# One last block moved ahead in GpSimd's queue, one output pair sent last, one input block evacuated in one go

## The chip, the cores and the metric

The kernel runs on 1 core of one Trainium2 chip. The metric is the time of one execution in microseconds of the device. Times quoted from the profile are from one profiled execution; all others are medians over runs.

The engines are named as in the profile: PE (TensorE, the matrix products), DVE (VectorE), ACT (ScalarE), POOL (GpSimd) and SP (the queue from which all large transfers of this kernel are issued). Each engine takes its instructions strictly in its own order.

## What is computed

A trunk of two layers over 1024 frames of 1024 features, in float32. Layer 0 runs a state-space branch with a gated linear unit and a retention branch side by side and maps both back; layer 1 is a convolution module. A normalization stands ahead of each layer and behind the last.

```python
def rmsnorm(x, g):
    y = x * rsqrt(mean(x * x, axis=-1) + EPS) * g

def mixer_conv(h, ...):                      # layer 1
    a, b, g = split(h @ w_in, 3)
    u = causal_depthwise_conv31(a * sigmoid(b)) + conv_b
    u = (u - mean(u)) * rsqrt(var(u) + EPS) * ln_g + ln_b
    return (silu(u) * silu(g)) @ w_out       # x = x + this; then the final rmsnorm
```

## The kernel before

Features lie on the 128 partitions, so a 1024x1024 matrix is eight feature blocks (`nb` or `kb`, 0 to 7); frames lie along the free axis, in two halves (`h`, 0 and 1) of 512. A float32 product is made of three faster ones: every operand is split into a high part (`zh`, `wh`, rounded) and a low part (`zl`, `wl`, what the rounding left), and `mm3` adds high by high (L181), low by high (L182) and high by low (L183). One output block of one half is thus 24 matmuls in one of three PSUM banks.

Instructions are put in order by a scheduler that works with priorities (`self.at(number)`) and with orders written by hand: under `issue_after(x)` an instruction comes behind `x` in the order. Such a line adds no wait on the chip by itself between instructions of one engine; it only fixes the queue.

Three places matter here.

- **Front.** `u_block(nb)` (L351) takes the first projection out of PSUM: `evac` (L354) multiplies a half of 512 frames by the normalization factor `R` and writes it into the tile `ut`, once for each half, on DVE. The finished `ut` (two buffers) is sent to DRAM as `u_d[nb]` by L364. The PSUM bank is free when `evac` is done, and the buffer of `ut` is free again when its transfer has landed; block 2 uses the buffer of block 0. The products of blocks 0, 1 and 2 are already made when `R` is ready, so their evacuations come together.
- **Last normalization of layer 1.** For each feature block of half 1, `conv_scale` (L1612) does: scale by the normalization factor (L1626), subtract the scaled mean (L1631), SiLU on ACT (L1632), multiply by the gate `gl` (L1641), high part on ACT (L1235), low part (L1237). Blocks 3, 5 and 7 are done by POOL on the tiles `co`, the others by DVE on tiles `zz` in PSUM. The last product (`w_out_c`, tiles `mm_oc`) of half 1 needs all eight blocks. The same function adds, for half 0, the squares of its finished blocks on POOL (L1678, tile `s2q`); their sum goes through PE (L487, `rf_R`) into the final normalization of half 0. In the order by hand, the additions for blocks 5, 6 and 7 of half 0 come behind the low part of block 3 (`third_low`), and the scaling of block 7 comes behind the low part of block 5.
- **End.** `final_norm` (L1684) multiplies the last 256 frames by their factor and sends them in pairs of feature blocks (L1712), in the order 4-5, 0-1, 2-3, 6-7 of the loop; 4-5 is done by POOL, the other three pairs by DVE.

Of the kernel before, what the change touches and what calls it, by code (L numbers as in the profile page):

```python
# [15 lines left out]
ALU = mybir.AluOpType  # L16
# [3 lines left out]
P = 128  # L20
# [32 lines left out]
class Trunk:  # L53
# [190 lines left out]
    def layer0_front(self, st):  # L244
        tc, nc, A = self.tc, self.nc, self.A
# [36 lines left out]
        for kb in range(KB):  # L282
            t = xt[kb] = ev.tile([P, T], F32, name=f"x_{kb}", tag="xin", bufs=8)
# [67 lines left out]
        def u_block(nb):  # L351
            ut = uv.tile([P, 8, P], F32, name=f"ut_{nb}", tag="ut", bufs=2)

            def evac(h, ps):  # L354
                r = self.R[:, h * HALF:(h + 1) * HALF]
                self.u_evac[nb] = nc.vector.tensor_tensor(
                    ut[:, ::-1, h * 64:(h + 1) * 64], ps[:].rearrange("p (m j) -> p j m", j=8),
                    r.rearrange("p (m j) -> p j m", j=8), op=ALU.mult)
# [5 lines left out]
            nc.sync.dma_start(self.u_d[nb].rearrange("j h g m -> (h g) j m"), ut[:])  # L364
# [874 lines left out]
    def layer0_back_and_layer1(self, st):  # L1239
        nc, A = self.nc, self.A  # L1240
# [101 lines left out]
        for i, x in ((6, t2), (7, t3), (4, t4)):  # L1342
            for m in range(2):
# [268 lines left out]
        def conv_scale(h, Rp, dl):  # L1612
            R, steps = None, {}

            def behind(nb, step, of):

                ins = steps.get((nb - 2, of)) if h and nb in (5, 7) else None
                return self.tc.issue_after(ins.ins) if ins else nullcontext()

            for nb in range(8):  # L1620
                c = cv[h][nb]

                e1, e = (v, gp) if h == 0 else (gp, gp) if nb in (3, 5, 7) else (v, v)
                z = ps_cv.tile([P, HALF], F32, name=f"zz{nb}_{h}", tag="cv") if e is v else c
                with behind(nb, "scale", "sub" if nb == 5 else "low"):
                    e1.tensor_tensor(z[:], c[:], (R if e1 is gp else Rp)[:], op=ALU.mult)  # L1626
                if h and nb == 0:
                    R = lp.tile([P, HALF], F32, name=f"RL_{h}", tag="cq", bufs=1)
                    nc.scalar.copy(R[:], Rp[:])
                with behind(nb, "sub", "gate"):  # L1630
                    steps[nb, "sub"] = e.tensor_tensor(z[:], z[:], dl[:], op=ALU.subtract)  # L1631
                silu = nc.scalar.activation(z[:], z[:], AF.Silu, scale=self.vec(V_LNG, nb), bias=self.vec(V_LNB, nb))  # L1632
                if nb == 0:
                    self.first_silu = silu
                tag, bufs = ("ld", 2) if h == 0 else ("tp", 3) if nb < 3 else ("u", 5)
                g = lp.tile([P, HALF], F32, name=f"gl{nb}_{h}", tag=tag, bufs=bufs)

                with self.tc.issue_after(self.low_load["ca1"].ins) if h == 0 and nb < 2 else nullcontext():
                    nc.sync.dma_start(g[:], self.gs_d[rows(nb), hs(h)])
                with behind(nb, "gate", "low" if nb == 7 else "gate"):  # L1640
                    steps[nb, "gate"] = e.tensor_tensor(z[:], g[:], z[:], op=ALU.mult)  # L1641
# [10 lines left out]
        def w_out_c(h, nb, cols, hold=None):  # L1652

            w = self.wnext(f"woc{nb}_{h}")
            tag, bufs = ("tp", 3) if h and nb > 4 else ("ld", 2)
            xt = lp.tile([P, HALF], F32, name=f"x1l{nb}_{h}", tag=tag, bufs=bufs)
            with self.tc.issue_after(self.early_low.ins) if h and nb > 4 else nullcontext():
                nc.sync.dma_start(xt[:], self.x1_d[rows(nb), hs(h)])
            t = self.opA.tile([P, HALF], F32, name=f"x2_{nb}_{h}", tag=f"A{h}")
            sq = lp.tile([P, HALF], F32, name=f"s2q{nb}_{h}", tag="sacc" if nb == 0 else "ev",  # L1660
                         bufs=1 if nb == 0 else 3)
            final[h].append((t, sq))

            def part(c):
                ps = self.bank(f"mm_oc{nb}_{h}_{c.start}", aux=False)
                n = c.stop - c.start
                self.gemm(ps[:, :n], w, [(a[:, c], b[:, c]) for a, b in zs[h]], hold)
                behind = self.behind.pop(nb, None)
                with self.tc.issue_after(behind.ins) if behind else nullcontext():
                    self.last_add = v.tensor_tensor(t[:, c], ps[:, :n], xt[:, c], op=ALU.add)  # L1670

                with self.tc.issue_after(self.halved.ins) if h == 0 and nb >= N0 else nullcontext():
                    self.squared = nc.scalar.activation(sq[:, c], t[:, c], AF.Square)

                if 0 < nb < KB - (h == 1 and c.start > 0):
                    a = final[h][0][1]
                    with self.tc.issue_after(self.third_low.ins) if h == 0 and nb > 4 else nullcontext():
                        gp.tensor_tensor(a[:, c], a[:, c], sq[:, c], op=ALU.add)  # L1678
                with self.tc.issue_after(self.squared.ins):
                    nc.scalar.mul(t[:, c], t[:, c], self.vec(V_FG, nb))  # L1680
            for c in cols:
                yield part(c)

        def final_norm(h, c):  # L1684
            n = c.stop - c.start
            end = h and c.stop == HALF
# [8 lines left out]
            R = lp.tile([P, HALF], F32, name=f"RF_{h}_{c.start}", tag="dg", bufs=1)  # L1695
            for nb in (4, 5, 0, 1, 2, 3, 6, 7) if end else range(8):
                if nb == 4:
                    yield
# [2 lines left out]
                t = final[h][nb][0]  # L1701
                e = gp if (nb // 2 == 2 if end else nb % 3 == 2) else v
                c0 = h * HALF + c.start
# [5 lines left out]
                    o = lp.tile([P, 2, n], F32, name=f"fo{nb}_{c0}", tag="u", bufs=5)  # L1709
                e.tensor_tensor(o[:, nb % 2, :], t[:, c], (R if e is gp else rp)[:, :n], op=ALU.mult)  # L1710
                if nb % 2:
                    nc.sync.dma_start(self.out[(nb - 1) * P:(nb + 1) * P, c0:c0 + n]  # L1712
                                      .rearrange("(b p) t -> p b t", b=2), o[:])

        with self.at(100000):
            w_out(0, range(8))
# [176 lines left out]
```

## Time and profile before

| | |
|---|---|
| median of 3 runs | 1181.32 us (1181.07 to 1181.44) |
| the profiled execution, its own time | 1181.03 us |
| its span, first to last instruction | 1179.2 us |
| PE busy | 1168.7 us, 99% of the span |
| DVE, POOL, ACT busy | 850.8, 654.2, 489.0 us |
| mean granted TensorE clock | 0.998 |

How to read the views: a row of the timeline has its start and its length in us from the start of the span, then engine, line of the code, operation, tile written `<-` tiles read, shape and count; in brackets how long the engine had been idle before, and what ended that. A row with x2 or more merges neighbours. Matmuls overlap: each is shown for 0.39 us or so, but the next starts about 0.23 us after it. DVEq, SPq and the like are an engine's sequencer.

### The profile page before, as it was taken

To read this page: it belongs to the slowest core of one execution; us is meant where nothing else is said; L and a number is where in the kernel's file an instruction comes from. 1 tells how busy PE (TensorE), PEld (TensorE's weight loads), DVE (VectorE), ACT (ScalarE), POOL (GpSimd) and SP (SyncE) were. 2 spreads that over 40 slices of the span, in tenths; PEclk is the share of its full clock that TensorE was granted. 3 is DMA by queue.
4 is the path that set the end of the run, shared out by engine and by line. 5 is a ranking of instruction groups with operands and counts; after the bars stand their busy time and mean duration, and the time that the engine had idled before them with its cause. 6 is when DMAs were issued, how large, how long until landed. Compare 5 with 4: busy or idle time off the path is not lost.

```text
span 1179.2 us, 17214 instructions
## 1 busy us (share of the span) xinstructions
PE 1168.7 (99%) x6286; PEld 978.4 (83%) x6286; DVE 850.8 (72%) x1464; ACT 489.0 (41%) x719; POOL 654.2 (55%) x448
## 2 busy tenths in 40 slices
PE   9999999999999999999999999999999999999997
PEld 7888888888888888999888888888888888888776
DVE  7975698777417359586679333599999899899834
ACT  6322232322223231333456324455536675444763
POOL 2059999888145344232673111588534567677653
PEclk9999999999999999999999999999999999999999
DMA  9344355555387667769998977656678554357854
GB/s 356 105 134 137 124 150 170 182 176 170 135 275 266 245 219 208 260 210 346 382 344 278 340 262 250 218 193 214 205 259 277 214 181 167 117 191 265 273 203 166
DMA packets 117637, 261.46 MB, mean 222 GB/s; under 512 B 10672, under 2 KB 42288, under 8 KB 116912
## 3 DMA queue, kind: packets, MB, share of 16 engines
q1 hardware_dynamic: 117552, 260.36, 65.6%
q8 instruction: 49, 0.80, 0.3%
q14 instruction: 36, 0.29, 0.1%
HBM read 181.48 MB, written 74.65 MB: 217 GB/s over the span
## 4 chain that ended last, share of the span: by engine, by line
PE 96%; POOL 1%; ACT 1%; DVE 1%; issue 1%; DMA 1%; POOLq 0%; SPq 0%; ACTq 0%
PE mm_g L181 8%; PE mm_g L183 7%; PE mm_g L182 7%; PE mm_wo L182 5%; PE mm_wo L183 5%; PE mm_wo L181 5%; PE mm_b L183 2%; PE mm_b L182 2%; PE mm_a L182 2%; PE mm_b L181 2%; PE mm_a L181 2%; PE mm_a L183 2%; PE mm_u L183 2%; PE mm_u L181 2%; PE mm_u L182 2%; PE mm_glu L181 2%
## 5 line engine op out<-in xcount | busy, mean ns | idle before, releaser
L1508 DVE SCALAR_TENSOR_TENSOR cv<-u,convw,cv 128x512 f32<-128x512 f32 x398 | 273.1, 749 | 11.6 <-ACT cv L1487 9.7
L1481 POOL TENSOR_TENSOR tp<-tp,tp 128x512 f32<-128x512 f32 x64 | 83.8, 1309 | 36.6 <-ACT tp L1480 35.6
L181 PE MATMUL mm_g<-xh,wh_g 128*128 128x512 f32 x256 | 101.8, 398 | 0.0
L183 PE MATMUL mm_g<-xh,wl_g 128*128 128x512 f32 x256 | 100.2, 391 | 0.0
L182 PE MATMUL mm_g<-xl,wh_g 128*128 128x512 f32 x256 | 100.1, 391 | 0.0
L415 POOL TENSOR_TENSOR s1q<-s1q,s1q 128x512 f32<-128x512 f32 x12 | 17.7, 1477 | 85.4 <-ACT s1q L410 85.4
L1480 ACT ACTIVATE tp<-u,convw 128x512 f32<-128x512 f32 x64 | 45.3, 719 | 34.3 <-POOL tp L1481 34.2
L181 PEld LDWEIGHTS mm_g<-xh,wh_g 128*128 128x128 f32 x256 | 48.0, 188 | 11.7 <-issue 1.2
L183 PEld LDWEIGHTS mm_g<-xh,wl_g 128*128 128x128 f32 x256 | 48.1, 188 | 10.4
L182 PEld LDWEIGHTS mm_g<-xl,wh_g 128*128 128x128 f32 x256 | 48.1, 188 | 9.9 <-issue 0.4
L371 DVE TENSOR_TENSOR gt<-mm_g,R 128x512 f32<-128x512 f32 x32 | 21.8, 683 | 44.1 <-PE mm_g L183 44.1
L182 PE MATMUL mm_oc<-zl,wh_woc 128*128 128x512 f32 (+1 forms) x144 | 52.6, 367 | 0.4 <-POOL zl L1237 0.4
L181 PE MATMUL mm_oc<-zh,wh_woc 128*128 128x512 f32 (+1 forms) x144 | 52.2, 374 | 0.5 <-ACT zh L1235 0.5
L183 PE MATMUL mm_oc<-zh,wl_woc 128*128 128x512 f32 (+1 forms) x144 | 52.5, 367 | 0.0
L172 POOL TENSOR_TENSOR wl_v<-wf_v,wh_v 128x1024 fp32r<-128x1024 f32 x12 | 31.0, 2583 | 38.7 <-ACT wh_v L171 38.7
L172 POOL TENSOR_TENSOR wl_glu<-wf_glu,wh_glu 128x1024 fp32r<-128x1024 f32 x14 | 34.0, 2430 | 32.9 <-ACT wh_glu L171 27.1
L181 PE MATMUL mm_g<-h1h,wh_cg 128*128 128x512 f32 x128 | 50.2, 392 | 0.0
L181 PE MATMUL mm_wo<-ysh,wh_wos 128*128 128x512 f32 x128 | 50.2, 392 | 0.0
L183 PE MATMUL mm_b<-h1h,wl_cb 128*128 128x512 f32 x128 | 50.0, 391 | 0.0
L182 PE MATMUL mm_b<-h1l,wh_cb 128*128 128x512 f32 x128 | 49.8, 389 | 0.0
L182 PE MATMUL mm_wo<-ysl,wh_wos 128*128 128x512 f32 x128 | 49.8, 389 | 0.0
L181 PE MATMUL mm_b<-h1h,wh_cb 128*128 128x512 f32 x128 | 49.8, 389 | 0.0
(526 smaller groups left out, 3652.7 us busy)
## 6 DMA issues: line engine op xcount, KB each, us to landing
wf_g<-w_ab SPq DMA_DIRECT2D x16, 512.0 KB
wf_wos<-w_out SPq DMA_DIRECT2D x16, 512.0 KB
wf_wor<-w_out SPq DMA_DIRECT2D x16, 512.0 KB
wf_cb<-w_c SPq DMA_DIRECT2D x16, 512.0 KB
wf_ca<-w_c SPq DMA_DIRECT2D x16, 512.0 KB
wf_woc<-w_out_c SPq DMA_DIRECT2D x16, 512.0 KB
wf_v<-w_v SPq DMA_DIRECT2D x12, 512.0 KB
wf_cg<-w_c SPq DMA_DIRECT2D x11, 512.0 KB
```

The lines of the kernel that those rows point to most:

```text
L172: self.low_made = lo[i].tensor_tensor(wl[:].rearrange(fl)[:, c], wf[:, c], h.bitcast(F32), op=ALU.subtract)
L181: nc.tensor.matmul(ps, wh[:, kb, :], xh, start=start, stop=False, **more)
L182: nc.tensor.matmul(ps, wh[:, kb, :], xl, start=False, stop=False, **more)
L183: self.last_mm = nc.tensor.matmul(ps, wl[:, kb, :], xh, start=False, stop=stop, **more)
L371: nc.vector.tensor_tensor(gt[:, c], ps[:], self.R[:, c], op=ALU.mult)
L415: nc.gpsimd.tensor_tensor(a, a, sq[:], op=ALU.add)
L1480: nc.scalar.mul(sk[:], u[:, k:k + HALF], cw[:, nb, k:k + 1])
L1481: gp.tensor_tensor(s0[:], s0[:], sk[:], op=ALU.add)
L1508: v.scalar_tensor_tensor(dst[:], *tap, accs_[i][:], op0=ALU.mult, op1=ALU.add)
```

## The change

It changes four orders and no arithmetic; the number of instructions of each engine is the same.

- Front: the two evacuations of block 1 come behind the second one of block 0. In the built order DVE has block 0 half 0, block 0 half 1, block 1 half 0, block 1 half 1; before it had the halves 0 of both blocks, then the halves 1. The evacuation of block 2 also stands two small instructions (L591) further ahead.
- Block 7 on POOL: its scaling comes behind block 5's subtraction instead of behind its low part, and its subtraction is no longer held by hand. The three additions of squares come behind the low part of block 7 (`last_low`) instead of that of block 3. The built order of POOL, with the block in brackets, is

```
before: ... sub[5] gate[5] low[3] add add low[5] scale[7] add sub[7] gate[7] low[7]
after:  ... sub[5] scale[7] sub[7] gate[5] low[3] low[5] gate[7] low[7] add add add
```

  On ACT the SiLU of block 7 moves from behind the high part of block 6 to behind the SiLU of block 4, ahead of a multiplication of half 0, the SiLU of block 6 and the high parts of blocks 4, 5 and 6.
- On PE, in the last product of half 1, the three output blocks 0, 1 and 2 first take the high part of block 6 and only then its low parts; the number of matmuls is the same. The matmul L487 of half 0 stands behind the same matmuls as before, and now waits for additions that come last on POOL.
- End: the pair 4-5 is sent behind the other three. SP's last four transfers are 0-1, 2-3, 6-7, 4-5; before they were 0-1, 4-5, 2-3, 6-7.

```diff
             def evac(h, ps):
                 r = self.R[:, h * HALF:(h + 1) * HALF]
-                self.u_evac[nb] = nc.vector.tensor_tensor(
-                    ut[:, ::-1, h * 64:(h + 1) * 64], ...
+                with self.tc.issue_after(self.u_evac[0].ins) if nb == 1 else nullcontext():
+                    self.u_evac[nb] = nc.vector.tensor_tensor(
+                        ut[:, ::-1, h * 64:(h + 1) * 64], ...
...
-                with behind(nb, "scale", "sub" if nb == 5 else "low"):
+                with behind(nb, "scale", "sub"):
                     e1.tensor_tensor(z[:], c[:], (R if e1 is gp else Rp)[:], op=ALU.mult)
...
-                with behind(nb, "sub", "gate"):
+                with behind(nb, "sub", "gate") if nb == 5 else nullcontext():
                     steps[nb, "sub"] = e.tensor_tensor(z[:], z[:], dl[:], op=ALU.subtract)
...
                 steps[nb, "low"] = self.split(z[:], a, b, e)
-                if nb == 3:
-                    self.third_low = steps[nb, "low"]
+                if nb == 7:
+                    self.last_low = steps[nb, "low"]
...
-                    with self.tc.issue_after(self.third_low.ins) if h == 0 and nb > 4 else nullcontext():
+                    with self.tc.issue_after(self.last_low.ins) if h == 0 and nb > 4 else nullcontext():
                         gp.tensor_tensor(a[:, c], a[:, c], sq[:, c], op=ALU.add)
...
                 if nb % 2:
-                    nc.sync.dma_start(self.out[...], o[:])
+                    pair = self.out[...], o[:]
+                    if end and nb == 5:
+                        late = pair
+                    else:
+                        sent = nc.sync.dma_start(*pair)
+            if late:
+                with self.tc.issue_after(sent.ins):
+                    nc.sync.dma_start(*late)
```

More of the change, by code (lines that the diff above doesn't have):

```diff
@@ L355, in evac @@
                 r = self.R[:, h * HALF:(h + 1) * HALF]
-                self.u_evac[nb] = nc.vector.tensor_tensor(
-                    ut[:, ::-1, h * 64:(h + 1) * 64], ps[:].rearrange("p (m j) -> p j m", j=8),
-                    r.rearrange("p (m j) -> p j m", j=8), op=ALU.mult)
+                with self.tc.issue_after(self.u_evac[0].ins) if nb == 1 else nullcontext():
+                    self.u_evac[nb] = nc.vector.tensor_tensor(
+                        ut[:, ::-1, h * 64:(h + 1) * 64], ps[:].rearrange("p (m j) -> p j m", j=8),
+                        r.rearrange("p (m j) -> p j m", j=8), op=ALU.mult)
             if nb < 3:
@@ L1695, in final_norm @@
             R = lp.tile([P, HALF], F32, name=f"RF_{h}_{c.start}", tag="dg", bufs=1)
+            late = sent = None
             for nb in (4, 5, 0, 1, 2, 3, 6, 7) if end else range(8):
@@ L1711, in final_norm @@
                 if nb % 2:
-                    nc.sync.dma_start(self.out[(nb - 1) * P:(nb + 1) * P, c0:c0 + n]
-                                      .rearrange("(b p) t -> p b t", b=2), o[:])
+                    pair = self.out[(nb - 1) * P:(nb + 1) * P, c0:c0 + n].rearrange("(b p) t -> p b t", b=2), o[:]
+                    if end and nb == 5:
[5 more added lines that the diff above has]
+                    nc.sync.dma_start(*late)
         with self.at(100000):
```

## The prediction

> **What bounds the kernel now.** I read the page's busy times first, then the waits of PE alone, then the timeline at each place where PE waits.
>
> ```profile
> PE 1168.7 (99%) x6286; PEld 978.4 (83%) x6286; DVE 850.8 (72%) x1464; ACT 489.0 (41%) x719; POOL 654.2 (55%) x448
> ```
>
> ```profile
> PE idle L273 <- DVE mhalf L218: 1.1, 1, 1.1
> PE rf_ps L444 <- ACT s2q L1673: 0.6, 1, 0.6
> PE mm_oc L181 <- ACT zh L1235: 0.5, 1, 0.5
> PE mm_u L181 <- DVE ut L356: 0.4, 1, 0.4
> PE mm_oc L182 <- POOL zl L1237: 0.4, 1, 0.4
> PE mm_u L181 <- ACT wh_u L171: 0.4, 1, 0.4
> PE cst L487 <- DVE cq L1594: 0.4, 1, 0.4
> ```
>
> PE is busy for 99% of the span, so other engines' busy times decide nothing; what they cost is in the few places where PE stands. The list is complete as the view has it, 3.8 us together. Three belong to code that the change touches: PE waiting for the evacuation `ut` (front), for the high part of a block (L181, `zh` by ACT) and for a low part (L182, `zl` by POOL). A fourth piece of time lies behind the last matmul, where outputs are sent. So the change is worth at most those pieces, unless it makes a new wait.
>
> **Front.** The view is the timeline of DVE, SP and PE around 48 us.
>
> ```profile
> 40.97 2.24 DVE L356 TENSOR_TENSOR ut<-mm_u,R 128x512 f32<-128x512 f32 x2
> ...
> 43.22 2.18 DVE L356 TENSOR_TENSOR ut<-mm_u,R 128x512 f32<-128x512 f32 x2
> ...
> 46.52 0.65 DVE L591 SCALAR_TENSOR_TENSOR s5t<-s5t,s5t 128x32 f32<-128x32 f32 x3
> 47.51 2.16 DVE L356 TENSOR_TENSOR ut<-mm_u,R 128x512 f32<-128x512 f32 x2 [0.34 <-DMA u_d<-ut]
> 44.40 1.40 SPq L364 DMA_DIRECT2D u_d<-ut  x2
> 47.95 0.39 PE L183 MATMUL mm_u<-xh,wl_u 128*128 128x512 f32 x1
> 48.77 0.47 PE L181 MATMUL mm_u<-xh,wh_u 128*128 128x512 f32 x1 [0.43 <-DVE ut L356]
> 49.07 0.40 PE L182 MATMUL mm_u<-xl,wh_u 128*128 128x512 f32 x1
> ```
>
> The first two evacuations (40.97) are the halves 0 of blocks 0 and 1, the next two (43.22) the halves 1. One takes about 1.12 us with the next behind it 1.05 us later. Block 0 is complete when the third ends, at 44.3, and its transfer is issued at 44.40. Block 2 needs the same buffer: its evacuation starts at 47.51, after 0.34 us of idling that this transfer ended, so it landed 3.1 us after its issue. PE needs the bank that this evacuation frees. PE's matmuls start about 0.227 us apart, so the one at 48.77 was due at 48.18: 0.59 us late, and the start after it (49.07) comes 0.30 behind instead of 0.227, another 0.07. The stall costs 0.67 us.
>
> After the change block 0 is complete when the second evacuation ends, one pitch (1.05) earlier; issue 43.35, landing 3.1 later at 46.45. On DVE block 2 then stands behind the fourth evacuation (same time, only two swapped), one weight split and one L591 (row of three, 0.65, so 0.22 each): from 46.52 on one such, start 46.75. That is 0.3 behind the landing. The first evacuation of block 2 ends at 47.87, the bank is taken 0.14 later (48.77 less the end 48.63 before), at 48.0, and PE is due at 48.18. The stall goes: **0.67 us**, with 0.17 to spare. What is late next is nothing near: the swapped evacuations of block 1 free banks outside PE's three, and the order of DVE's small parameter work shifts by tenths.
>
> Does this carry on to the end? PE's next wait in the list is `cst` for DVE's `cq`, at the end of the convolution, where DVE is full. It carries if DVE itself follows PE there.
>
> ```profile
> 1085.81 0.69 DVE L1670 TENSOR_TENSOR x<-mm_oc,x1l 128x512 f32<-128x512 f32 x1 [0.80 <-PE mm_oc L183]
> ```
>
> DVE idled 0.80 us for PE's product here, within the last 20 us ahead of `cst`. With PE 0.67 earlier DVE starts 0.67 earlier even if nothing of its own backlog moved, and 0.13 of idling is left. So I take all of it.
>
> **Block 7.** The view is the timeline of POOL, ACT and PE.
>
> ```profile
> 1122.60 1.30 POOL L1641 TENSOR_TENSOR co<-gl,co 128x512 f32<-128x512 f32 x1 [2.24 <-ACT co L1632]
> 1124.17 1.29 POOL L1237 TENSOR_TENSOR zl<-co,zh 128x512 fp32r<-128x512 f32 x1 [0.28 <-ACT zh L1235]
> 1125.41 2.68 POOL L1678 TENSOR_TENSOR s2q<-s2q,s2q 128x512 f32<-128x512 f32 x2
> 1128.04 1.29 POOL L1237 TENSOR_TENSOR zl<-co,zh 128x512 fp32r<-128x512 f32 x1
> 1129.29 1.29 POOL L1626 TENSOR_TENSOR co<-co,RL 128x512 f32<-128x512 f32 x1
> 1130.54 1.30 POOL L1678 TENSOR_TENSOR s2q<-s2q,s2q 128x512 f32<-128x512 f32 x1
> 1131.80 1.29 POOL L1631 TENSOR_TENSOR co<-co,dl 128x512 f32<-128x512 f32 x1
> 1134.02 1.29 POOL L1641 TENSOR_TENSOR co<-gl,co 128x512 f32<-128x512 f32 x1 [0.93 <-ACT co L1632]
> 1136.04 1.28 POOL L1237 TENSOR_TENSOR zl<-co,zh 128x512 fp32r<-128x512 f32 x1 [0.73 <-ACT zh L1235]
> ```
>
> ```profile
> 1123.93 0.75 ACT L1632 ACTIVATE zz<-zz,vecs 128x512 f32<-128x512 f32 x1
> ...
> 1126.36 0.63 ACT L1235 CAST zh<-co 128x512 fp32r<-128x512 f32 x1
> ...
> 1133.12 0.82 ACT L1632 ACTIVATE co<-co,vecs 128x512 f32<-128x512 f32 x1 [5.64 <-POOL co L1631]
> ```
>
> ```profile
> 1131.97 0.39 PE L182 MATMUL mm_oc<-zl,wh_woc 128*128 128x512 f32 x1
> ...
> 1135.14 0.39 PE L183 MATMUL mm_oc<-zh,wl_woc 128*128 128x512 f32 x1
> 1136.01 0.96 PE L181 MATMUL mm_oc<-zh,wh_woc 128*128 128x512 f32 x3 [0.48 <-ACT zh L1235]
> 1137.37 0.50 PE L182 MATMUL mm_oc<-zl,wh_woc 128*128 128x512 f32 x1 [0.40 <-POOL zl L1237]
> ...
> 1138.89 1.02 PE L487 MATMUL rf_R<-s2q,ones 128*128 128x512 f32 x2
> ```
>
> POOL is the path: two additions (1125.41), block 5's low part (1128.04), scaling of block 7 (1129.29), the third addition, subtraction (1131.80); SiLU on ACT (1133.12), gate (1134.02), high part on ACT, low part (1136.04, end 1137.32). PE meets block 7 in the matmul at 1136.01 and its low part at 1137.37. From 1131.97 to 1135.14 are 14 starts in 3.17 us, 0.2265 each. From 1135.14 to `rf_R` at 1138.89 are 10 starts, due in 2.27, taken 3.75: both stalls and the slow starts behind them cost **1.48 us**.
>
> After the change: POOL idled 2.24 us ahead of the row at 1122.60, that is from 1120.36. Scaling and subtraction of block 7 fall into this hole: with 1.25 and 1.37 from start to end (1.29 an operation, a little more where one waits for the other) they end at about 1122.98, so gate 5 starts 0.35 later than 1122.60 and ends at 1124.25; low part 3 waits for ACT until 1124.17 anyway, and loses 0.1 at most. On ACT the SiLU of block 7 stands behind that of block 4 (1123.93): its input is ready, it takes 0.82 (row 1133.12) and nothing but its own length is added to what is queued behind it (a multiplication of half 0, the SiLU of block 6, the high parts of 4, 5, 6). Block 5's high part then ends at 1126.36 + 0.82 + 0.63 = 1127.81. POOL's queue behind it: low part 5 from 1127.95 (before 1128.04, so PE's first use of it at 1131.97 is safe), gate 7 to 1130.5, high part 7 on ACT to 1131.2, low part 7 to about 1132.6. PE comes to block 7 at 1135.14 + 0.23 = 1135.37 and to its low part at 1136.05: spare 4.2 and 3.4 us.
>
> The price is the new wait of `rf_R`: the three additions now come last, 2.68 for two and so 1.34 each, 4.0 together, end 1136.6. PE is there at 1135.14 + 2.27 = 1137.41. They are covered by 0.8 us; everything that PE has queued behind `rf_R` (the rest of half 1) would wait if they came later than that, microsecond for microsecond. So 1.48 us, of which I count 1.45 for a semaphore's delay somewhere in it.
>
> PE's changed order inside the three output blocks delays the use of block 6's low parts, by no additional matmul: nothing. The swap moves no transfer into SP's queue at this place.
>
> **End.** The view is the timeline, then the windows of 1 us (the last two columns: share of DMA time, GB/s), then SP's waits.
>
> ```profile
> 1172.33 2.08 DVE L1710 TENSOR_TENSOR fo<-x,rf_R 128x256 f32<-128x256 f32 x6 [0.79 <-PE rf_R L483]
> 1173.21 1.41 POOL L1710 TENSOR_TENSOR fo<-x,RF 128x256 f32<-128x256 f32 x2 [3.74 <-ACT RF L1700]
> 1174.65 1.43 SPq L1712 DMA_DIRECT2D outT<-fo  x3
> ```
>
> ```profile
> 1174.00:1175.00 1.00, 0.00 (x0) 0.00 (x0) 0.41 (x2) 0.00 (x0) 0.62 (x1) 1.00 0.77 261
> 1175.00:1176.00 1.00, 0.00 (x0) 0.00 (x0) 0.00 (x0) 0.00 (x0) 0.00 (x0) 0.64 0.43 142
> ```
>
> ```profile
> SPq L1889 <- DMA outT<-fo: 2.1, 3, 0.7
> ```
>
> SP sends 0-1 and then stands for POOL's pair, which is ready at 1174.62; only then go 4-5, 2-3 and 6-7, from 1174.65, one each 0.48 us (three in 1.43, to 1176.08, the last at 1175.60). DVE's six multiplications, 0.35 apart, had 2-3 ready at about 1173.74 and 6-7 at 1174.41. In the windows the transfers stand still for 0.23 + 0.57 = 0.80 us between the first pair and the other three, and the final waits (2.1 us for three) show these landing 0.7 apart, one behind the other. After the change 2-3 goes at 1173.77, 6-7 at 1174.44, 4-5 at 1174.92. Each is there before its predecessor's 0.7 to 0.8 us of transfer are over, so the hole is filled: **0.80 us**. From below the last issue alone moves by 1175.60 - 1174.92 = 0.68. From above, if transfers did not queue: the last issue plus the 2.1 that 4-5 took (1174.65 to the first of the three waits, 1176.08 + 0.7) is 1177.0 against a last landing at 1176.08 + 2.1 = 1178.2, 1.2 us. I take 0.80, since the three landings one behind the other show a queue. Nothing is queued behind the pair that now goes last.
>
> The Trainium skill (DMA: Bandwidth & Descriptors, section Anatomy of one DMA, whose fit is for another issuing path than SP's) gives a transfer about 2.0 us fixed and its bytes over 436 GB/s, without queueing; by that only the last issue counts, and the term would be 0.68, the sum 2.80. The landings one behind the other speak for the larger one.
>
> **Sum.** 0.67 + 1.45 + 0.80 = 2.92 us off the profiled execution's 1181.03 (its span and 1.8 around it, which the change leaves alone), 1178.11. The median shown, 1181.32, is 0.29 above that execution; from it the forecast is 1181.32 - 2.92 = **1178.4 us**, 0.25% faster. About 0.2%, 2.4 us or a time of 1178.96, is what a measurement of this kernel can tell from no change, so the forecast is just beyond it.
>
> **Rivals.**
>
> *The front's gain is eaten* at `cst`: DVE's convolution, not PE, sets that moment. For it: PE waits for DVE there (0.4 in the list). Against: the idling of 0.80 for PE shortly ahead of it. Price 0.67, time 1179.1.
>
> *Half of block 7 stays*: ACT's queue, with one SiLU more in front of three high parts, lets PE wait in between or delays POOL by more than worked out. For it: one ACT row of 0.82 stands in front of work that POOL waits for. Against: spare times of 3 us. Price 0.7, time 1179.1.
>
> *The pair sent last changes nothing*, because the writes' rate and not the hole sets the last landing. Against: the hole of 0.80 itself. Price 0.8, time 1179.2.
>
> *Slower: the additions behind block 7 hold `rf_R`.* If block 7's chain is not paced by POOL's order (a late gate tile, ACT's queue), its low part comes late and the additions 4.0 later still. Should it end at 1137.32 as before, `rf_R` starts at 1141.3 instead of 1138.89, 2.4 late, and with the gains at the front and the end the time is 1181.32 + 2.4 - 0.67 - 0.80 = 1182.3. It costs from an end of 1133.4 on (1137.41 - 4.0), and the kernel is slower than before from 1136.4 on. Worked out is 1132.6; against it speaks that every part ahead of it in the queue has its row here, and that the gate tile of block 7 is read without waiting for a transfer at 1134.02 before.
>
> **How the numbers follow.** The forecast has 0.75; the front eaten 0.09; half of block 7 0.06; the end without gain 0.04; slower 0.06. The forecast's own range is 0.67 + 1.48 + 1.2 = 3.35 off, 1178.0, and the runs' spread of 0.2 to 0.4, so 1177.8, up to 1178.9 (half a microsecond less gained, as by a late semaphore or a transfer). The range to hold 8 times in 10 takes in the three cases at 1179.1 to 1179.2 with a little spread: 1177.8 to 1179.5. Faster by over 0.2%: the forecast but for a corner of it, 0.71. Within 0.2%: that corner, the three partial cases and half of the slower one, 0.26. Slower by over 0.2%: 0.03.
>
> **What would show it.** Right: PE's waits lose `mm_u <- DVE ut` and both `mm_oc` lines; the evacuation of block 2 starts at about 46.75 without idling for `u_d`; POOL's low part of block 7 ends about 5 us earlier relative to PE, with three additions behind it and no `rf_R <- POOL`; SP's last four issues run without a long gap, and the DMA share of the last microseconds has no hole. Wrong: a PE wait at `rf_R L487` for POOL, a longer wait at `cst`, or a last landing no earlier relative to the last multiplication.

## The result, and the profile after

The changed kernel took 1178.62 us (median of 14 runs, 1177.87 to 1179.6) beside 1181.38 for the kernel before (14 runs in turn with it, 1181.07 to 1185.29). The ratio on record is 0.9974, with a 95% interval of 0.9965 to 0.9982: 0.26% faster. Forecast were 1178.4 us and a range of 1177.8 to 1179.5. The profiled execution took 1178.34 us, its span is 1176.5 against 1179.2, and the mean granted clock is 0.999.

The page's line of busy times and PE's waits, which are again complete as the view has them:

```profile
PE 1168.5 (99%) x6286; PEld 979.8 (83%) x6286; DVE 844.5 (72%) x1464; ACT 489.9 (42%) x719; POOL 655.3 (56%) x448
```

```profile
PE idle L273 <- DVE mhalf L218: 1.1, 1, 1.1
PE rf_ps L446 <- ACT s2q L1675: 0.6, 1, 0.6
PE cst L489 <- DVE cq L1596: 0.4, 1, 0.4
```

Busy times say nothing, as before: the same work, PE at 99%. In the list of waits the line `mm_u <- DVE ut` and both lines `mm_oc` are gone, and there is none for `rf_R`. The wait at `cst` is still 0.4. The line `mm_u <- ACT wh_u` is gone as well, but that is no work of the change: it lies at 6 us, ahead of all that was edited, and in the second trace of the same kernel (e4 below) it is there with 0.5. (Lines of the code are now numbered up to 11 higher: L356 is L358, L1678 is L1680, L1710 is L1713.)

**Front**, timeline of DVE, SP and PE:

```profile
41.50 1.13 DVE L358 TENSOR_TENSOR ut<-mm_u,R 128x512 f32<-128x512 f32 x1
...
42.65 3.22 DVE L358 TENSOR_TENSOR ut<-mm_u,R 128x512 f32<-128x512 f32 x3
...
47.12 2.16 DVE L358 TENSOR_TENSOR ut<-mm_u,R 128x512 f32<-128x512 f32 x2
43.82 2.45 SPq L366 DMA_DIRECT2D u_d<-ut  x2
48.49 0.39 PE L183 MATMUL mm_u<-xh,wl_u 128*128 128x512 f32 x1
48.71 0.39 PE L181 MATMUL mm_u<-xh,wh_u 128*128 128x512 f32 x1
48.94 0.39 PE L182 MATMUL mm_u<-xl,wh_u 128*128 128x512 f32 x1
```

By 46 us this execution is 0.54 us later than that of the profile before (below), so 0.54 is to be taken off to compare. Block 2's evacuation starts at 47.12, or 46.58, without the bracket `<-DMA u_d<-ut`. Its first half ends at 48.24 (one evacuation takes 1.12). PE's matmul that was 0.59 late before starts on its pitch, 0.22 behind its predecessor.

**Block 7**, timeline of POOL, ACT and PE:

```profile
1119.91 1.30 POOL L1628 TENSOR_TENSOR co<-co,RL 128x512 f32<-128x512 f32 x1
1121.29 1.29 POOL L1633 TENSOR_TENSOR co<-co,dl 128x512 f32<-128x512 f32 x1
1122.54 1.29 POOL L1643 TENSOR_TENSOR co<-gl,co 128x512 f32<-128x512 f32 x1
1123.80 1.28 POOL L1239 TENSOR_TENSOR zl<-co,zh 128x512 fp32r<-128x512 f32 x1
1127.39 1.30 POOL L1239 TENSOR_TENSOR zl<-co,zh 128x512 fp32r<-128x512 f32 x1 [2.31 <-ACT zh L1237]
1128.65 1.29 POOL L1643 TENSOR_TENSOR co<-gl,co 128x512 f32<-128x512 f32 x1
1130.67 1.29 POOL L1239 TENSOR_TENSOR zl<-co,zh 128x512 fp32r<-128x512 f32 x1 [0.73 <-ACT zh L1237]
1131.92 4.01 POOL L1680 TENSOR_TENSOR s2q<-s2q,s2q 128x512 f32<-128x512 f32 x3
1124.22 0.81 ACT L1634 ACTIVATE co<-co,vecs 128x512 f32<-128x512 f32 x1
1134.87 0.84 PE L181 MATMUL mm_oc<-zh,wh_woc 128*128 128x512 f32 x3
1135.55 0.39 PE L182 MATMUL mm_oc<-zl,wh_woc 128*128 128x512 f32 x1
...
1136.92 1.02 PE L489 MATMUL rf_R<-s2q,ones 128*128 128x512 f32 x2
```

Scaling and subtraction of block 7 (1119.91, 1121.29) fill the hole of 2.24 us that POOL had ahead of block 5's multiplication by the gate; the SiLU on ACT follows at 1124.22 instead of 1133.12. The low part of block 7 ends at 1131.96, and PE comes to it at 1135.55 (its row of three high parts at 1134.87 runs at full pitch, without a bracket). The three additions end at 1135.93, 0.99 ahead of `rf_R`.

**End**, timeline, windows of 1 us (last two columns: share of DMA time, GB/s) and SP's final waits:

```profile
1170.39 2.08 DVE L1713 TENSOR_TENSOR fo<-x,rf_R 128x256 f32<-128x256 f32 x6 [0.79 <-PE rf_R L485]
1171.27 1.41 POOL L1713 TENSOR_TENSOR fo<-x,RF 128x256 f32<-128x256 f32 x2 [3.75 <-ACT RF L1703]
1171.17 1.70 SPq L1720 DMA_DIRECT2D outT<-fo  x3
1172.96 0.45 SPq L1723 DMA_DIRECT2D outT<-fo  x1
```

```profile
1172.00:1173.00 1.00, 0.00 (x0) 0.00 (x0) 0.47 (x2) 0.00 (x0) 0.68 (x1) 1.00 0.93 313
1173.00:1174.00 1.00, 0.00 (x0) 0.00 (x0) 0.00 (x0) 0.00 (x0) 0.00 (x0) 1.00 1.01 334
1174.00:1175.00 1.00, 0.00 (x0) 0.00 (x0) 0.00 (x0) 0.00 (x0) 0.00 (x0) 0.68 0.99 350
1175.00:1176.00 1.00, 0.00 (x0) 0.00 (x0) 0.00 (x0) 0.00 (x0) 0.00 (x0) 0.50 0.15 51
```

```profile
SPq L1899 <- DMA outT<-fo: 2.1, 3, 0.7
```

SP no longer stands between its issues for longer than a pair takes to become ready. Worked out from the shares of the first and the last window, the transfers run from 1172.07 to 1175.15 without a hole: 3.08 us for four pairs of 256 KB, 0.77 each.

**How the three places are priced in every run.** All traces here have 6286 matmul rows on PE, so the n-th start on PE can be set against the n-th start in the trace before. The difference at a matmul is how much later (+) or earlier (-) the execution is by then; what it changes by across a stretch is what that stretch gained. The stretches, in the clock of the kernel before: front, 47.95 to 60.20; blocks, 1135.14 to 1150.18; end, from the last spread of the normalization on PE (1171.60) to the end of the span. The table is worked out from the twelve traces of these kernels and that of before, and is in us, good to 0.01. The times of each set were taken in turn with the kernel before on the same chip (its medians: 1181.38, 1181.55 for e1 to e4, 1181.63 for e5 to e8, 1181.3 for e9 to e11), and the ratio, as on record, is against these runs; it differs a little from the quotient of the medians.

| kernel | front | blocks | end | median, us (lowest to highest, runs) | ratio, 95% interval |
|---|---|---|---|---|---|
| the change | -0.69 | -1.45 | -0.76 | 1178.62 (1177.87 to 1179.6, 14) | 0.9974 [0.9965, 0.9982] |
| e1 front alone | -0.70 | +0.02 | 0.00 | 1181.41 (1180.37 to 1187.3, 12) | 1.0002 [0.9992, 1.0012] |
| e2 block alone | -0.09 | -1.43 | 0.00 | 1180.49 (1180.04 to 1182.24, 11) | 0.999 [0.9982, 0.9999] |
| e3 end alone | -0.06 | -0.07 | -0.76 | 1180.59 (1179.83 to 1182.16, 11) | 0.9994 [0.9985, 1.0002] |
| e4 the change again | -0.70 | -1.47 | -0.77 | 1178.37 (1178.18 to 1180.92, 9) | 0.9975 [0.9965, 0.9984] |
| e5 move only | -0.70 | -1.43 | -0.76 | 1177.86 (1177.79 to 1178.32, 5) | 0.9968 [0.9956, 0.998] |
| e6 additions only | -0.70 | -0.66 | -0.78 | 1179.17 (1178.68 to 1180.25, 10) | 0.9977 [0.9967, 0.9988] |
| e7 pair sent third | -0.69 | -1.43 | -0.75 | 1178.64 (1178.05 to 1183.53, 7) | 0.9979 [0.9968, 0.999] |
| e8 first pair split | -0.70 | -1.42 | -0.91 | 1178.24 (1177.65 to 1179.85, 7) | 0.9974 [0.9963, 0.9984] |
| e9 additions only, order held | -0.70 | +0.41 | -0.77 | 1180.52 (1180.14 to 1181.39, 10) | 0.9991 [0.9982, 1.0] |
| e10 without the front | -0.06 | -1.47 | -0.78 | 1179.7 (1178.48 to 1180.97, 11) | 0.9986 [0.9977, 0.9995] |
| e11 move only and split | -0.69 | -1.45 | -0.90 | 1178.53 (1177.81 to 1181.1, 11) | 0.9979 [0.997, 0.9988] |

The three columns agree to within 0.09 wherever the code of that place is the same. The runs of one kernel spread by 0.5 us to several, so a term of 0.7 is read in the traces; the times can only agree.

For the change the three columns add up to 2.90 us. The spans differ by 2.7, because two things outside the edited places differ as well: the start of this execution was 0.54 later by 46 us, and a wait of about 0.3 us near 918 us, for a weight's low part, was in the trace before and not in this one (2.90 + 0.30 - 0.54 = 2.66). Neither belongs to the change: at 46 us the other executions stood anywhere between 0.75 later (e10) and 0.00 (e8), and near 918 us e1 and e3 were 0.30 shorter than the trace before too, e2 0.16 longer.

### The profile page after: what moved, and what is told of

Read it like the earlier page. It is cut to its first block, busy times and chain, and to the rows that moved or that the text cites. A ratio compares the mean times of both kernels' runs of the same rounds, so it can differ in the third digit from the quotient of the medians.

```text
span 1176.5 us, 17212 instructions
## 1 busy us (share of the span) xinstructions
PE 1168.5 (99%) x6286; PEld 979.8 (83%) x6286; DVE 844.5 (72%) x1464; ACT 489.9 (42%) x719; POOL 655.3 (56%) x448
## 4 chain that ended last, share of the span: by engine, by line
PE 98%; issue 0%; ACT 0%; POOL 0%; DVE 0%; POOLq 0%; ACTq 0%
PE mm_g L181 8%; PE mm_g L182 7%; PE mm_g L183 7%; PE mm_wo L182 5%; PE mm_wo L183 5%; PE mm_wo L181 5%; PE mm_b L183 2%; PE mm_b L182 2%; PE mm_a L183 2%; PE mm_a L182 2%; PE mm_b L181 2%; PE mm_a L181 2%; PE mm_oc L183 2%; PE mm_u L182 2%; PE mm_oc L181 2%; PE mm_oc L182 2%
```

## The experiments

**e1, e2, e3: each part alone; e4: all three again.** The edits are the three parts of the diff of the change, each alone put into the kernel before (main lines only):

```diff
 e1, evac():
+                with self.tc.issue_after(self.u_evac[0].ins) if nb == 1 else nullcontext():
 ...
 e2, conv_scale() and the additions of squares:
-                with behind(nb, "scale", "sub" if nb == 5 else "low"):
+                with behind(nb, "scale", "sub"):
-                with behind(nb, "sub", "gate"):
+                with behind(nb, "sub", "gate") if nb == 5 else nullcontext():
-                if nb == 3:
-                    self.third_low = steps[nb, "low"]
+                if nb == 7:
+                    self.last_low = steps[nb, "low"]
 ...
 e3, final_norm():
+                    if end and nb == 5:
+                        late = pair
 ...
```

> The kernel before with the reordered evacuations alone. Theory: the profile loses the PE wait of the matmul for `ut` at 48 us (0.67 us with its slow restart), the evacuation of block 2 does not idle for the transfer of block 0, the two `mm_oc` waits near 1136 us stay (1.48 us together) and so does the 0.80 us hole in the last transfers; time 0.67 us below the kernel before, about 1180.7. Rival (eaten at the end of the convolution): the PE wait goes at 48 us, but the wait of `cst` for `cq` grows from 0.35 to about 1.0 us and the time stays at that of the kernel before.

> The kernel before with the move of block 7 and of the three additions alone. Theory: the two `mm_oc` waits go, 1.48 us, no wait of `rf_R` for POOL, the last low part on POOL ends about 5 us earlier and the additions end about 1 us before PE comes to `rf_R`; time about 1179.9. Rival (additions hold `rf_R`): a PE wait there, and a gain under 1 us or none.

> The kernel before with the order of the last four transfers alone. Theory: the hole of 0.80 us in the last transfers closes; from the start of the last six multiplications on DVE to the end of the span 6.15 us instead of 6.90, time 0.75 us below the kernel before, about 1180.6. Rival (rate of the writes sets the end): same length behind the last multiplications, no gain.

> The changed kernel once more, unchanged, on the chip of the three parts. Theory (the three parts add up): its gain is the sum of those of the three parts, 2.9 us, within the spread of the runs of about 0.5 us. Rival (one part's gain is lost where the others are present, or two gain the same time): sum and whole differ by more than that. Its profile also shows how much the first 40 us, which no part touches, differ from one execution to another (0.5 us between the two profiles so far).

Each part brings its own term in its own place and less than 0.1 in the other two: 0.70, 1.43 and 0.76, together 2.89, and the change run again has 0.70, 1.47 and 0.77. So in the traces the parts are additive, and no part lives off another. The times cannot show this. Against 1181.55, the median of before on that chip, e1 is 0.14 lower, e2 1.06 and e3 0.96, together 2.2, where e4 is 3.2 lower: a difference of more than the 0.5 that was allowed for e4, but each of these figures has an interval of about 1 us to either side. The interval of e3 reaches past 1, and in that of e1 (ratio 1.0002) a gain of 0.7 cannot be seen. In e2 the block's 1.43 is there in the trace too, but its profiled execution ends with the span of the kernel before (1179.2): it began 0.65 later, and lost 0.68 more between 200 and 400 us, where its list of waits has 0.4 for `mm_v` (a weight's low part by POOL), in code that the change leaves alone.

**e10: the change without its front.** Because e1's times could not tell, the front was also taken out of the whole.

```diff
-                with self.tc.issue_after(self.u_evac[0].ins) if nb == 1 else nullcontext():
-                    self.u_evac[nb] = ...
+                self.u_evac[nb] = ...
 ...
```

> The changed kernel with the front's edit alone taken back. Theory: the front is worth 0.6 to 0.7 us also in the presence of the other two, the PE wait mm_u for DVE ut of 0.4 is there again, and PE is 0.6 to 0.7 later behind 60 us and remains so to the end; time about 1179.1. Rival (the front's gain is eaten at cst): the wait at cst is 0.4 with the front and lasts under 0.4 without it, and the time stays at 1178.4 to 1178.6. The runs of one kernel spread over 0.5 to 1 us, so the trace is to decide and the times only to agree.

Two of its waits, and its timeline:

```profile
PE mm_u L181 <- DVE ut L356: 0.4, 1, 0.4
PE cst L487 <- DVE cq L1594: 0.4, 1, 0.4
```

```profile
48.21 2.15 DVE L356 TENSOR_TENSOR ut<-mm_u,R 128x512 f32<-128x512 f32 x2 [0.35 <-DMA u_d<-ut]
...
49.47 0.47 PE L181 MATMUL mm_u<-xh,wh_u 128*128 128x512 f32 x1 [0.39 <-DVE ut L356]
```

The chain of the prediction is back as it was: DVE stands 0.35 for the transfer `u_d`, PE 0.39 for DVE. The front's column falls from -0.69 to -0.06. The time is 1179.7, 1.2 above that of e11 below, which was taken in turn with it and has the front (1178.53); the intervals of the two ratios still overlap, so the trace decides. The wait at `cst` is 0.4 with the front and 0.4 without it: it doesn't eat the front's gain.

**e5, e6: the two halves of the block's edit.** The first leaves the additions where they were, the second leaves scaling and subtraction where they were; everything else is the change.

```diff
 e5:
-                if nb == 7:
-                    self.last_low = steps[nb, "low"]
+                if nb == 3:
+                    self.third_low = steps[nb, "low"]
 ...
 e6:
-                with behind(nb, "scale", "sub"):
+                with behind(nb, "scale", "sub" if nb == 5 else "low"):
-                with behind(nb, "sub", "gate") if nb == 5 else nullcontext():
+                with behind(nb, "sub", "gate"):
```

> The changed kernel with one step taken back: the three additions of squares stand again behind the third low part, only scaling and subtraction of block 7 are ahead of block 5's low part. What it tells apart: whether the gain at block 7 needs both halves of the edit. My theory: the moved scaling and subtraction bring it, because they use POOL's idling (2.24 us in the profile of before) and let ACT's SiLU go early; the additions are only pushed out of a queue that has room. In the clock of the changed kernel's profile: low part 3 ends at 1125.1, two additions end at 1127.7, block 5's low part ends at 1129.0 (PE uses it 3 us later), gate 7 at 1130.3, third addition at 1131.5, low part of block 7 at 1132.8, with PE due there at 1135.55. So no wait for it, the stretch across the three blocks keeps its 1.47 us, and the additions end at 1131.5 instead of 1135.93, 5.4 ahead of rf_R instead of 0.99. Rival: the gain comes from the additions going out of the way; then block 7's low part is late again and 0.4 to 1.5 us return as PE mm_oc waits. Time by my theory 1178.4 (ratio to before 0.9975), by the rival 1178.8 to 1179.9.

> The changed kernel with the other step taken back: scaling and subtraction of block 7 stand again behind block 5's low part, the three additions behind block 7's low part. This makes the slower rival's case on purpose, and tests its threshold: additions that end after PE is at rf_R cost microsecond for microsecond. In the clock of the changed kernel's profile: block 5's low part ends at about 1127.9, scaling 1129.1, subtraction 1130.4, SiLU 1131.25, gate 1132.6, high part 1133.25, low part of block 7 at 1134.6 (PE due at 1135.55, no wait), three additions of 4.0 end at 1138.6, PE at rf_R at 1136.92 if undisturbed. Theory: a wait of rf_R for POOL of 1.6 to 1.8 us, so this place loses all of its 1.47 and a little more; time about 1180.1 (0.9989). Rival: PE has other work to put there or the additions are short enough, the wait is under 0.5; time 1178.5 to 1178.9.

Timeline of POOL in e5:

```profile
1125.08 2.68 POOL L1680 TENSOR_TENSOR s2q<-s2q,s2q 128x512 f32<-128x512 f32 x2
1127.71 1.29 POOL L1239 TENSOR_TENSOR zl<-co,zh 128x512 fp32r<-128x512 f32 x1
...
1130.20 1.31 POOL L1680 TENSOR_TENSOR s2q<-s2q,s2q 128x512 f32<-128x512 f32 x1
1131.46 1.30 POOL L1239 TENSOR_TENSOR zl<-co,zh 128x512 fp32r<-128x512 f32 x1
```

In e5 the low part of block 7 ends at 1132.76, 0.8 later than in the changed kernel and still 2.8 ahead of PE (the same 1135.55). The stretch keeps its 1.43. So the early scaling and subtraction are enough for the gain; that the additions go behind block 7 as well adds nothing, and takes their cover ahead of `rf_R` from 5.4 us (they end at 1131.51) down to 0.99. The median of e5, 1177.86, is 0.8 below that of the change, but it comes from five runs, the intervals overlap, and the trace has no such gain.

In e6 the expected wait did not come. Timeline of POOL, ACT and PE:

```profile
1133.06 1.28 POOL L1239 TENSOR_TENSOR zl<-co,zh 128x512 fp32r<-128x512 f32 x1 [0.73 <-ACT zh L1237]
1135.30 0.39 PE L182 MATMUL mm_oc<-zl,wh_woc 128*128 128x512 f32 x1
1134.31 4.03 POOL L1680 TENSOR_TENSOR s2q<-s2q,s2q 128x512 f32<-128x512 f32 x3
1135.73 2.95 ACT L148 CAST wh_woc<-wf_woc 128x1024 fp32r<-128x1024 f32 x3 [2.74 <-PE mm_oc L182]
1137.78 0.50 PE L181 MATMUL mm_oc<-zh,wh_woc 128*128 128x512 f32 x1 [0.21 <-ACT wh_woc L148]
1143.37 1.02 PE L489 MATMUL rf_R<-s2q,ones 128*128 128x512 f32 x2
```

Two things are to be read here. First, block 7 is in time by this half too: its low part ends at 1134.34, 0.96 ahead of PE (1135.30), and neither `mm_oc` wait of before is there. Putting the additions behind block 7 takes them out of POOL's queue ahead of it, and that alone frees the same 1.4 us. So either half of the edit removes the two waits, and neither was needed beside the other.

Second, this half has a price when it stands alone. The additions end at 1138.34, close to the 1138.6 worked out, but `rf_R` is at 1143.37: in the built order it stands behind 26 more matmuls. The scheduler had put it there; why is not shown. PE pays something else: the weights of the next output blocks, which ACT makes from 1135.73 on (`wh_woc`), are now wanted at once instead of behind `rf_R`. The matmul starts at 1136.84 and 1137.78 are 0.18 and 0.38 late, each with 0.11 more behind it, together 0.78. That is the difference of the column, -0.66 against -1.45. So late additions cost 0.78 by this way, and not the 1.6 to 1.8 expected; the rival's "other work to put there" was right about PE's order and wrong on the price.

**e9: e6 with PE's order held.** The following block's matmuls are put behind `rf_R` by hand.

```diff
-                blocks(1, range(3, 6))
+                blocks(1, range(3, 6), {3: {0: self.last_stat}})
```

> The kernel of adds only, with PE's order held as in the changed kernel: the matmuls of half 1's output blocks 3 to 5 stand behind the sums rf_R, so that the sums cannot be put behind 26 of them as they were in adds only. It separates two accounts of why late additions cost 0.78 us there and not 1.7: that the place of rf_R in PE's order was moved out of their way (and 0.78 was the price of PE meeting the next block's weights early), or that additions which end late do not hold PE at all. In the clock of adds only: the additions end at 1138.34, PE is due at rf_R at 1136.92 - 0.25 = 1136.67. By the first account a wait of rf_R for POOL of 1.7 to 1.8 us and no wait for wh_woc; the stretch across the three output blocks gains nothing against the kernel before (-1.47 + 1.75 = +0.3), time about 1180.2. By the second the wait is under 0.5 and the time about 1178.6.

Waits and timeline:

```profile
PE rf_R L489 <- POOL s2q L1680: 1.6, 1, 1.6
```

```profile
1134.79 4.00 POOL L1680 TENSOR_TENSOR s2q<-s2q,s2q 128x512 f32<-128x512 f32 x3
...
1138.84 1.12 PE L489 MATMUL rf_R<-s2q,ones 128*128 128x512 f32 x2 [1.62 <-POOL s2q L1680]
```

`rf_R` starts 0.05 behind the additions' end (1138.79), 1.78 later than its pitch, and no weight is waited for. With the next start 0.10 late as well, the stretch loses 1.86 against the change (+0.41 against -1.45), where 1.75 was expected. Block 7 itself is again in time, without an `mm_oc` wait. This is the case of the prediction's slower rival, and its rule held in it: additions that ended 1.73 after PE was due cost 1.78 and the late start behind, with PE's order held. The whole kernel is still at 0.9991 (the interval reaches 1.0), because front and end keep their 1.47.

**e7: the pair 4-5 sent third.**

```diff
-                        sent = nc.sync.dma_start(*pair)
-            if late:
-                with self.tc.issue_after(sent.ins):
-                    nc.sync.dma_start(*late)
+                        with self.tc.issue_after(sent.ins) if sent else nullcontext():
+                            sent = nc.sync.dma_start(*pair)
+                        if end and nb == 3:
+                            with self.tc.issue_after(sent.ins):
+                                sent = nc.sync.dma_start(*late)
```

> The changed kernel with the pair 4-5 sent third instead of last (0-1, 2-3, 4-5, 6-7). It separates two accounts of the end. POOL's pair is ready at 1172.68 in the changed kernel's profile, so 4-5 would be issued at 1172.71 and 6-7 at 1173.19, while now the last issue is at 1172.96. If the last issue sets the last landing, the end comes 0.23 us later. If the four transfers are a queue that is never empty (0.77 each from 1172.07 on), nothing changes: the third would be due to begin at 1173.6, 0.9 after its issue, the fourth at 1174.38, 1.2 after its issue. I expect the queue: from the last PE matmul to the end of the span the same within 0.1 as in the changed kernel, no hole in the DMA share. Time 1178.4.

Timeline of SP's queue and windows:

```profile
1172.61 0.37 SPq L1724 DMA_DIRECT2D outT<-fo  x1
1173.08 0.45 SPq L1721 DMA_DIRECT2D outT<-fo  x1
```

```profile
1173.00:1174.00 1.00, 0.00 (x0) 0.00 (x0) 0.00 (x0) 0.00 (x0) 0.00 (x0) 0.90 0.98 324
1174.00:1175.00 1.00, 0.00 (x0) 0.00 (x0) 0.00 (x0) 0.00 (x0) 0.00 (x0) 0.50 1.02 350
```

PE's last matmuls are 0.10 earlier here than in the changed kernel, so the last issue (1173.08) is 0.22 later in relation to them. The end column is -0.75 against -0.76: nothing was lost, and the DMA share has no hole. The last issue does not set the end: the transfers are one queue, and here an issue has only to come early enough for its first data, about 0.9 us later, to be there when its predecessor is through. The change alone could not tell this, since its last issue and its end moved by nearly the same (0.7 and 0.76).

The Trainium skill (DMA: Bandwidth & Descriptors, section Anatomy of one DMA, a fit for transfers issued from GpSimd) prices one transfer by a fixed part and its bytes; counted from the last issue, that would put the last landing 0.22 later. The trace has 0.01, so for these transfers behind one another on SP's queue the price of one alone does not give the end.

**e8: the first pair sent as two single blocks.** If the transfers are a queue, an earlier first one should bring its whole advance.

```diff
+                if end and nb < 2:
+                    sent = nc.sync.dma_start(self.out[rows(nb), c0:c0 + n], o[:, nb, :])
+                    continue
```

> The changed kernel with the first pair sent as two single blocks, 0 and then 1. Block 0 is ready at 1170.74 in the changed kernel's profile, one multiplication (0.35) ahead of the pair, so the first transfer starts 0.3 to 0.4 earlier (issue 1170.76 instead of 1171.17, first data about 0.9 behind it), and the last issue stays at 1172.96. Queue theory: the transfers are one behind the other from the first data on, so the end comes 0.3 to 0.4 us earlier. If the last issue sets it: nothing. From below, two smaller transfers may take longer together than one of 256 KB: up to 0.3 of the gain lost. I expect 0.3 earlier, time 1178.1; in the times hardly to be told from the changed kernel, in the profile from the last matmul to the end of the span.

Timeline of SP's queue, and windows of 0.25 us:

```profile
1170.30 0.82 SPq L1715 DMA_DIRECT2D outT<-fo  x2
1171.29 1.04 SPq L1723 DMA_DIRECT2D outT<-fo  x2
```

```profile
1171.00:1171.25 0.25, 0.00 (x0) 0.00 (x0) 0.25 (x2) 0.00 (x0) 0.25 (x1) 1.00 0.32 111
...
1171.50:1171.75 0.25, 0.00 (x0) 0.00 (x0) 0.25 (x2) 0.00 (x0) 0.25 (x1) 1.00 0.63 201
...
1172.00:1172.25 0.25, 0.00 (x0) 0.00 (x0) 0.00 (x0) 0.00 (x0) 0.13 (x1) 0.50 0.30 86
```

The end column is -0.91, 0.15 better than the change, where 0.3 to 0.4 was expected. The first data comes at 1171.17; this execution is 0.54 ahead of the changed kernel's here, so that is 0.36 earlier than its 1172.07, as expected. But two holes open behind it: 0.37 of the slice from 1171.50 and 0.70 of the slice from 1172.00 are empty, 0.09 and 0.17 us. The first lies between the two single blocks. The second lies ahead of the pair 2-3, which is issued at 1171.29, when DVE has finished it, with its data about 0.9 later like that of the other stores here. More than half of what the first transfer gained is given back there: what holds the end next is when DVE has a pair ready.

**e11: e5 and e8 together.** This is the version to which the experiments point: the additions back with their large cover, and the first pair split.

> The changed kernel with the additions of squares back behind the third low part (as in move only) and the first pair sent as two single blocks (as in split). By the profiles of those two: the same 1.47 us at the three blocks with the additions 5.4 us ahead of rf_R, and 0.1 us less at the end than in the changed kernel, since the first data comes 0.28 earlier but blocks 2-3 are ready too late to follow at once. Time 1178.0 to 1178.3, not to be told from the changed kernel by the times. If the two work on each other, the end or the blocks' stretch differs by more than 0.1 from those figures.

Its columns are -0.69, -1.45 and -0.90, the sum of its parts as expected. Its time, 1178.53, is not to be told from the change (ratios to before 0.9979 [0.997, 0.9988] and 0.9974 [0.9965, 0.9982]). By the traces it has 0.14 us less at the end, and the additions end 5.6 us ahead of `rf_R` (1136.56 against an end of 1130.97) instead of 0.99; a better version by its reserve, not by a time that was shown.

## Why the prediction was right, point by point

- **The sum**: 2.92 us were predicted from three terms; the traces have 2.90 (and 2.94 in e4), term by term within 0.05. The median came out 2.76 lower (1181.38 to 1178.62).
- **Front**, predicted 0.67, measured 0.69 and 0.70. The chain was named rightly: `u_d`'s landing, DVE's evacuation, PE's bank. Block 2's evacuation was placed at 46.75 and started at 46.58, because the small instruction ahead of it (L593, L591 before) takes 0.10 from start to start (47.02 to 47.12) and not the 0.22 put in. The bank is free some 0.3 ahead of PE (48.24 + 0.14 against 48.71) instead of 0.17. When `u_d` landed the views no longer show, since nothing waits for it.
- **Carried to the end**: the 0.67 was let through on the strength of DVE idling 0.80 for PE at 1085.81 (here 0.79 at 1085.41). The rival, that `cst` eats it, fell by e1 and e10: the wait there is 0.4 with and without the front, and in e1 PE loses nothing of its lead from 60 us to the last matmul.
- **Block 7**, predicted 1.45 (1.48 worked out), measured 1.42 to 1.47. The steps agree in the order as printed: low part 5 from 1127.95 (here 1127.39, or 1127.89 with the 0.50 by which this execution is ahead there), end of block 7's low part 1132.6 (1131.96, or 1132.46), end of the additions 1136.6 (1135.93, or 1136.43). The cover ahead of `rf_R` was put at 0.8 and was 0.99. What the prediction had not seen is that the edit does the same thing twice: by e5 the early scaling and subtraction are enough, and by e6 and e9 the additions' move alone frees block 7 as well, at the price that the slower rival names. The prediction set this price beside the gain without asking whether the gain needs it; e5 has the gain without it.
- **End**, predicted 0.80 between 0.68 and 1.2, measured 0.75 to 0.78 wherever the pair is late enough and the first pair is whole. The choice of the queue over the last issue was the right one (e7). Of the 0.04 that is missing, 0.02 is a reading: in quarter windows of the profile before, 0.07 of the slice from 1174.00 is empty, which is the first pair starting up and no part of the hole. The hole itself is 0.78.
- **The two other partial rivals** fell with it. ACT's longer queue cost what the prediction had put in: block 5's low part is where it was due, and no `mm_oc` wait is left. And the pair sent last brings its 0.76 alone as well (e3).
- **The slower rival**: its rule and its threshold held in e9. There the low part of block 7 ends at 1134.84, or 1135.19 in the clock of before (this execution is 0.35 ahead); with 4.0 for the additions and PE due at 1137.41 the rule gives 1.78, and 1.86 was lost. Without PE's order held by hand `rf_R` stood elsewhere, and the loss was 0.78 (e6). For the kernel as built, in which block 7's low part ended 1 us ahead of that threshold, it did not arise.
- **The median's distance to the profile** was taken from the runs before (0.29). It holds only within the spread of the runs: the start of an execution alone moved by 0.75 us among the traces. That the forecast came out at 0.2 from the median is in part luck.

## What to carry to other kernels

Price a reordering at the places where the bound engine stands, stretch by stretch, by setting the n-th instruction of that engine against the n-th of the trace before: terms of 0.7 us, which runs with a spread of 1 us cannot show, then repeat to some hundredths over many executions. An edit that moves two things should be halved, and both halves run: here either one freed block 7, so the second added nothing and only spent reserve, and which of them stands alone decides between no price (e5) and 0.78 or 1.86 us (e6, e9). And the transfers at the end of this kernel ended by their first data, their bytes and their holes, so no pair should wait in the queue behind one that becomes ready later.

## What had not been expected of the hardware

- The first 46 us of the same code took up to 0.75 us longer or shorter from one execution to another, with the code there unchanged, and single delays of 0.16 to 0.66 us came and went in the middle of the kernel: PE waiting for a weight's low part by POOL (0.66 in e2, 0.58 in e9) or from a transfer (0.16 in e2), and 0.21 in e4 for which the view names no wait.
- Behind a wait, the next start of PE also comes late, which the prediction had counted at two places: 0.31 instead of 0.227 at the front before, 0.34 in e6, and in e9 the second row of the sum 0.53 instead of 0.43 behind the first. A stall of PE cost 0.08 to 0.11 more than its length here.
- The sum `rf_R` is one matmul in the code, with operands that are not rounded, and two rows in the profile, 0.43 apart. The next product is shown only 0.03 behind the second row, and the one after it 0.63 later, in the traces of before, of the change, e5, e6, e9 and e11 alike, whether or not anything waited. Together these 0.66 are one 0.43 and one 0.23, so it can be that the second row takes its 0.43 too and the product between is shown early; no run here separates this from a late start.
- Stores of 256 KB on SP's queue ran at 334 and 350 GB/s in the two full windows of the change, 0.77 us a pair, with the first data about 0.9 us behind the start of the issue (1171.17 to 1172.07).
